# Retention scores per head over 64 rows in two banks, in place of zero-padded pairs

## The chip, the cores and the metric

One NeuronCore of one Trainium2 chip (1 of its 8) runs the whole block as a single program. The metric is device time in microseconds of one launch; lower is better.

## The reference

One layer of a hybrid backbone over 1024 tokens of width 1024, with 256 context tokens. One projection of the modulated, normalised input feeds two mixers, a gated long convolution (512 channels) and a retention with 8 heads of 64 channels in chunks of 128 tokens; their outputs go through one output projection, then a squared-ReLU MLP. The change lies in the retention:

```python
qc, kc, vc = ...            # (B, H, N chunks, C = 128, 64)
scores = jnp.einsum("bhncd,bhnmd->bhncm", qc, kc) * dmask[None, :, None]
out_inner = jnp.einsum("bhncm,bhnme->bhnce", scores, vc)
...
out_cross = jnp.einsum("bhncd,bhnde->bhnce", qc * w_q[None, :, None, :, None], s_prev)
return (out_inner + out_cross).reshape(B, H, L, dv)
```

## The kernel before, in words

The program is written with tiles drawn from pools; a scheduler orders the instructions of every engine by the tiles' dependencies, by priorities (`urgent()`, L187, raises one) and by when a buffer of a pool comes free. Nothing of the order around the change is written out by hand.

The stage in question comes in the middle of the run. Three kinds of work are interleaved in it. `split_mix` (L1051) loads the convolution's output (mraw), and splits it into a high and a low part (mx). `out_conv(d)` (L1060) projects it, 24 products of 512 columns per call into poh, written by `mm3` (L182 to 185), after which VectorE adds the result into XN (L1069). `retention(hh, n, ctr, gss)` (L1074) handles one chunk of 128 tokens for one group of four heads. It is called for hh in 0, 1 and n in 0 to 7, 16 chunks in all; behind every second chunk stands one call of `out_conv`, and behind every fourth a `group_norm` (L1120), whose transposes are pz and whose results mr. Later come the products por of the retention's half of the output projection; their weights are o2 and o3 (o3l is the low part of o3, made on VectorE at L1170).

One chunk of `retention` goes as follows. Four transposes (L1089) put q of four heads into the bank pqd. The input q2l holds each head's 64 channels twice (128 columns a head), so the transposed rows hold them in rows 0 to 63 and again in rows 64 to 127. VectorE multiplies the bank by the decay table into qw (L1092). ScalarE copies heads 0 and 2 into the upper 64 rows, heads 1 and 3 into the lower 64 rows of the buffer qz (L1094, L1095; it is part of sgqz), whose other halves were set to zero once, by two memsets (L1049). Two products of 128 rows and 256 columns (L1098) multiply the keys of a pair of heads (ktl, head 2p in rows 0 to 63, head 2p + 1 in rows 64 to 127) with it: the zeros keep the heads apart. The scores psc go through VectorE's mask multiply into sT (L1101). Sixteen products of half the columns (L1108) form the output po from sT and vtl and from qw and stl; VectorE takes the mean (mu, L1111), the centred values (ctrs, L1112) and, after ScalarE's square, the sums gss (L1116).

The PSUM banks come from pools with two buffers a tag: poh and por use the tag mm, pqd and psc the tag aux, po and pz the tag cv.

Of the kernel before, what the change touches and what calls it, by code (L numbers as in the profile page):

```python
# [13 lines left out]
ALU = mybir.AluOpType  # L14
# [3 lines left out]
P = 128  # L18
# [122 lines left out]
def tile_hymba_block(ctx: ExitStack, tc: tile.TileContext, I: dict, out: bass.AP, dbg=None, stop=99):  # L141
    nc = tc.nc
    V, A, G, PE, SP = nc.vector, nc.scalar, nc.gpsimd, nc.tensor, nc.sync
    dbg = dbg or (lambda name, ap: None)

    def bc(ap, k, shape):
        return ap.unsqueeze(k).broadcast_to(shape)
# [3 lines left out]
    def opool(key, bufs=1, **kw):  # L151
        st = ExitStack()
        es_open[key] = st
        return st.enter_context(tc.tile_pool(name=key, bufs=bufs, reuse_waits="tile", **kw))
# [21 lines left out]
    def ps_aux(name):  # L176
        return psB.tile([P, 512], F32, tag="aux", name=name)

    def ps_cv(name):
        return psB.tile([P, 512], F32, tag="cv", name=name)  # L180
# [6 lines left out]
    def urgent():  # L187

        return tc.high_priority(offset=6000)
# [52 lines left out]
    start = opool("start", side="right")  # L242
# [141 lines left out]
    for k in range(KC):  # L384
        for h in range(2):
# [9 lines left out]
            for i, (cv, w_) in enumerate(parts):  # L395
                for n in range(2):
                    PE.matmul(pga[h][0:4, n, :], lhsT=cv[:, k, :], rhs=w_[:, n * 512:(n + 1) * 512],  # L397
                              start=(k == 0), stop=(k == KC - 1 and i == 1))
# [120 lines left out]
    pr = ps_cv("prinv")  # L519
# [37 lines left out]
    def context(wh, wl, nm):  # L557
        ps = ps_aux(nm)
        pv = ps.rearrange("p (j n) -> p j n", n=256)
        for j in range(2):  # L560
            for k in range(KC):
                mm3(pv[:, j], hch[:, k, j * P:(j + 1) * P], hcl[:, k, j * P:(j + 1) * P],
                    wh[:, k], wl[:, k], k == 0, k == KC - 1)
        return pv
# [161 lines left out]
    wqT, msk = tab[:, 0], tab[:, 1]  # L726
# [15 lines left out]
    for hh in range(2):  # L742
        hs = slice(4 * hh, 4 * hh + 4)
        kr = kvp.tile([P, NCH, 256], F32, tag="kr", name=f"kr{hh}")
        wcur = slabs["k", hh]
        for g, ps in token_major(("k", hh), f"pk{hh}"):
# [4 lines left out]
            for m in range(2):  # L751
# [6 lines left out]
                kt = kvp.tile([P, 2, 256], F32, tag="kt", name=f"kt{hh}_{n0}")  # L758
                A.copy(kt.rearrange("p j n -> p (j n)"), pt)
                SP.dma_start(kT_d[hh][n0:n0 + 2].rearrange("j p n -> p j n"), kt)  # L760
        pc = context(*wcur, f"pck{hh}")
# [9 lines left out]
        for g, ps in token_major(("v", hh), f"pv{hh}"):  # L771
# [4 lines left out]
            for j in range(4):  # L776
                n = 4 * g + j
# [4 lines left out]
                for h in range(4):  # L782
                    for r in range(2):
                        PE.matmul(pt[64 * r:64 * r + 64, h * HD:(h + 1) * HD], lhsT=kw[:, h, r],
                                  rhs=vt[:, j, h * HD:(h + 1) * HD], start=True, stop=True)
                A.copy(Tt[0:64, n], pt[0:64, 0:256])
                A.copy(Tt[64:128, 7 - n], pt[64:128, 0:256])
        pc = context(*wcur, f"pcv{hh}")
# [4 lines left out]
        for h in range(4):  # L793
            for j in range(2):
                PE.matmul(pt[:, h * HD:(h + 1) * HD], lhsT=kwc[:, j, h].rearrange("p r d -> p (r d)"),
                          rhs=vc[:, j, h * HD:(h + 1) * HD], start=(j == 0), stop=(j == 1))
# [13 lines left out]
        for dr in range(2):  # L810
            rows = slice(64 * dr, 64 * dr + 64)
# [29 lines left out]
    for hv in range(2):  # L841
# [30 lines left out]
        for r, u in butterflies(cvp, scp, vT, 256, f"v{hv}"):  # L872
            nm = f"v{hv}{r}"
# [72 lines left out]
        for x, z in ((1, 7), (3, 5)):  # L946
            t = cvp.tile([P, 2, 256], F32, tag="pr1", name=f"sd{hv}{x}")
# [79 lines left out]
    def place(i, name, dt=F32R):  # L1027
        return big.tile([P, 4, 512], dt, tag=f"b{i}", name=name)
# [8 lines left out]
    wqT, msk = [tabq[:, 2 * i:2 * i + 2].rearrange("p a (h n) -> p (a h) n", n=P) for i in range(2)]  # L1037
# [3 lines left out]
    sgqz = place(12, "sgqz", F32)  # L1041
    sg = sgqz[:, 0:2].rearrange("p a n -> p (a n)").rearrange("p (j n) -> p j n", j=4)
    mraw = place(13, "mraw", F32)


    qz = [sgqz[:, 2 + i].rearrange("p (h n) -> p h n", h=4) for i in range(2)]
    with urgent():
        for t in qz:
            V.memset(t, 0.0)  # L1049

    def split_mix(k):  # L1051
        for q in range(2):
# [21 lines left out]
    def retention(hh, n, ctr, gss):  # L1074
        hs = slice(4 * hh, 4 * hh + 4)
        j = n % 4
        nm = f"{hh}_{n}"
        q2 = rtl.tile([P, 4, 2 * HD], F32, tag="q2", bufs=2, name=f"q2l{nm}")
        SP.dma_start(q2.rearrange("p h d -> p (h d)"), q2_d[hh][n])
        kt = rtl.tile([P, 2, P], F32, tag="ktl", bufs=2, name=f"ktl{nm}")  # L1080
        SP.dma_start(kt.rearrange("p a n -> p (a n)"), kT_d[hh][n])
        vt = rtl.tile([P, 256], F32, tag="vtl", bufs=2, name=f"vtl{nm}")
        SP.dma_start(vt, v_d[hh][n])
        st = rtl.tile([P, 256], F32, tag="stl", bufs=2, name=f"stl{nm}")
        SP.dma_start(st[0:64], st_d[hh][0, n])
        SP.dma_start(st[64:128], st_d[hh][1, 7 - n])
        pq = ps_aux(f"pqd{nm}")
        for h in range(4):
            PE.transpose(pq[:, h * P:(h + 1) * P], q2[:, h], ident)  # L1089
        pqv = pq.rearrange("p (h c) -> p h c", h=4)  # L1090
        qw = rtp.tile([P, 4, P], F32, tag="qw", bufs=2, name=f"qw{nm}")
        V.tensor_tensor(qw, pqv, wqT[:, hs], op=ALU.mult)  # L1092
        qT = qz[n % 2]
        A.copy(qT[0:64, 0:4:2], pqv[0:64, 0:4:2])  # L1094
        A.copy(qT[64:128, 1:4:2], pqv[64:128, 1:4:2])  # L1095
        pc = ps_aux(f"psc{nm}")
        for pr in range(2):
            PE.matmul(pc[:, pr * 256:(pr + 1) * 256], lhsT=kt[:, pr],  # L1098
                      rhs=qT[:, 2 * pr:2 * pr + 2].rearrange("p h c -> p (h c)"), start=True, stop=True)
        sT = rtp.tile([P, 4, P], F32, tag="sT", bufs=2, name=f"sT{nm}")  # L1100
        V.tensor_tensor(sT, pc.rearrange("p (h c) -> p h c", h=4), msk[:, hs], op=ALU.mult)  # L1101
        po = ps_cv(f"po{nm}")
        for h in range(4):
            cc = slice(h * HD, (h + 1) * HD)
            for w, o, first in ((sT, vt, True), (qw, st, False)):
                for r in range(2):
                    rows = slice(64 * r, 64 * r + 64)
                    PE.matmul(po[rows, cc], lhsT=w[:, h, rows], rhs=o[:, cc], start=first, stop=not first)  # L1108
        pov = po[:, 0:256].rearrange("p (h d) -> p h d", h=4)
        mu = rtp.tile([P, 4], F32, tag="mu", bufs=2, name=f"mu{nm}")  # L1110
        V.tensor_reduce(mu, pov, axis=AX.X, op=ALU.add)  # L1111
        V.scalar_tensor_tensor(ctr[:, j].rearrange("p (h d) -> p h d", h=4), bc(mu, 2, [P, 4, HD]), -1.0 / HD, pov,  # L1112
                               op0=ALU.mult, op1=ALU.add)
        sq = rtp.tile([P, 256], F32, tag="sqo", name=f"sqo{nm}")
        A.activation(sq, ctr[:, j], AF.Square)
        V.tensor_reduce(gss[:, j], sq.rearrange("p (h d) -> p h d", h=4), axis=AX.X, op=ALU.add)  # L1116
# [23 lines left out]
    for hh in range(2):  # L1140
        for g in range(2):
            ctr = ctrs[:, g]
            gss = rtp.tile([P, 4, 4], F32, tag="gss", bufs=2, name=f"gss{hh}{g}")
            for j in range(4):
                retention(hh, 4 * g + j, ctr, gss)
                if hh == 0 and g == 0 and j == 0:
                    for d in range(KC):
                        SP.dma_start(xn[d], I["xT"][d * P:(d + 1) * P])
                if j == 1 and pending:
                    group_norm(*pending)  # L1150
                if j == 1:
                    SP.dma_start(sg.rearrange("p n d -> p (n d)"), sg_d[hh][g])
                if j % 2:
                    out_conv(4 * hh + 2 * g + j // 2)
                if (hh, g, j) == (0, 0, 1):
                    prefetch()
                if (hh, g, j) == (0, 0, 3):
                    wo = [slab(I["w_out"][2], "o2", o2)]
                if (hh, g, j) == (1, 0, 0):

                    o3r = wpool.tile([P, 4, 512], F32, tag="wh", bufs=2, name="o3r")
                    SP.dma_start(o3r, I["w_out"][3])
            pending = hh, g, sg, ctr, gss
# [249 lines left out]
    def mlp1_step(f, c0, c1):  # L1413
        if f not in hid:
            if f % 2:
                hid[f] = [CH[:, i].rearrange("p (a n) -> p a n", a=2) for i in range(2)]
            else:
                hid[f] = [evs.tile([P, 2, 512], F32, tag=f"c{i}", name=f"c{i}_{f}") for i in range(2)]
        return dict(f=f, cols=slice(c0, c1), nm=f"1_{f}_{c0}")
# [4 lines left out]
    s = mlp1_step(0, 0, 256)  # L1424
# [5 lines left out]
    for f in range(NB):  # L1430
        with urgent():
            w1_load(f + 2)
        s = steps[f]
# [105 lines left out]
    for i, p in enumerate(TURNS[:-1]):  # L1539
        half, h = {1: (0, 0), 2: (0, 0), 5: (1, 1), 6: (0, 1), 3: (0, 1), 7: (1, 1)}[p]  # L1540
# [3 lines left out]
        for j in range(NG):  # L1544
            n = NG * i + j
            factors(n + AHEAD)
            t, w = TW.pop(n)
# [14 lines left out]
    n = NG * 6  # L1562
# [3 lines left out]
    for c, cols in enumerate(parts):  # L1566
        st = dict(ss=norms[0]["ss"][:, cols])
        for dp in range(4):
            db = slice(P * dp, P * dp + P)
            for j in range(NG):  # L1570
                t, w = TW[n + j]
# [25 lines left out]
```

## Time and profile before

| | |
|---|---|
| Time, three runs | 1373.8, 1377.99, 1381.97 us; median 1377.99 |
| Profiled execution | 1370.97 us, its span 1369.2 us |
| PE busy | 1294.8 us (95%) |
| VectorE (DVE) busy | 973.3 us (71%) |
| ScalarE (ACT) busy | 533.6 us (39%) |
| Retention stage, 15 of 16 chunks | 589.6 to 663.2 us |

How to read it: the times are of whole launches, the trace is of one of them. A row of a timeline gives start, duration, engine, line, operation and out<-in, with shapes; for matmuls "128\*128" is rows by columns of the array in use, and a product of f32 operands shows as two passes. Matmuls are pipelined, so a row's duration holds the way through the array; what a product takes from PE is the distance from its start to the next one's. A group of rows gives the count, the summed busy time and the mean of one in ns, then the idle time before them and what ended it.

### The profile page before, as it was taken

How to read it: one execution, taken by the hardware profiler on the slowest of the kernel's cores; microseconds unless marked ns; L12 is line 12 of the kernel's file. 1: busy time of each engine (PE TensorE's matmuls, PEld its weight loads, DVE VectorE, ACT ScalarE, POOL GpSimd, SP SyncE). 2: the span in 40 equal slices, each digit the busy share in tenths (PEclk: the TensorE clock that was granted, in tenths of full speed). 3: DMA queues.
4: the chain of work that ended last, by engine and by line, in shares of the span. 5: the costliest groups of instructions: out<-in, count | busy, mean ns of one | idle time of the engine just before them, and what ended most of it. 6: DMA issues, size and time to landing. Idle time of an engine off the chain costs nothing.

```text
span 1369.2 us, 20105 instructions
## 1 busy us (share of the span) xinstructions
PE 1294.8 (95%) x7386; PEld 1083.1 (79%) x7386; DVE 973.3 (71%) x1721; ACT 533.6 (39%) x912; POOL 19.4 (1%) x24
## 2 busy tenths in 40 slices
PE   6899899999999999799896999999998999999996
PEld 1479798988788999678776888888886888888896
DVE  5889787357878775558887988888656945555563
ACT  6863432213133121223455444444445744344420
POOL 0140000000000000000000000000000000000000
PEclk9799999999999999999998999999999999999999
DMA  9445766273536644776321789988636996666621
GB/s 374 175 151 160 233 206 212 79 228 129 169 120 215 206 162 155 270 243 182 104 96 64 251 306 326 348 302 300 238 123 232 338 321 190 193 201 185 199 79 62
DMA packets 139570, 278.19 MB, mean 203 GB/s; under 512 B 14672, under 2 KB 47056, under 8 KB 137040
## 3 DMA queue, kind: packets, MB, share of 16 engines
q1 hardware_dynamic: 137744, 272.19, 59.5%
q0 software_dynamic: 1152, 4.19, 0.8%
q8 instruction: 58, 0.95, 0.3%
q10 hardware_dynamic: 576, 0.52, 0.1%
q14 instruction: 40, 0.33, 0.1%
HBM read 193.75 MB, written 83.10 MB: 202 GB/s over the span
## 4 chain that ended last, share of the span: by engine, by line
PE 77%; DVE 8%; DMA 7%; ACT 4%; issue 2%; SPq 1%; POOL 0%; DVEq 0%; ACTq 0%; POOLq 0%
PE px L184 6%; PE px L185 6%; PE px L183 6%; PE pw L183 5%; PE py L183 5%; PE py L185 5%; PE py L184 5%; PE pw L185 5%; PE pw L184 5%; DMA dft_f_k<-in_dft_f 2%; PE pga L397 1%; PE pq L185 1%; PE pq L184 1%; PE pq L183 1%; PE pGv L901 1%
## 5 line engine op out<-in xcount | busy, mean ns | idle before, releaser
L1191 DVE TENSOR_TENSOR mt<-tr,mt 128x512 fp32r<-128x512 f32 x112 | 76.6, 688 | 99.6 <-ACT mt L1190 99.4
L1190 ACT CAST mt<-tr 128x512 fp32r<-128x512 f32 x112 | 69.6, 621 | 123.5 <-PE py L185 67.1
L183 PE MATMUL px<-mt,mw 128*128 128x512 f32 (+1 forms) x320 | 112.5, 352 | 3.0 <-ACT mw L1190 2.4
L184 PE MATMUL px<-mt,mw 128*128 128x512 f32 (+1 forms) x320 | 112.5, 352 | 0.7 <-DVE mt L1191 0.7
L185 PE MATMUL px<-mt,mw 128*128 128x512 f32 (+1 forms) x320 | 111.6, 350 | 0.0
L1191 DVE TENSOR_TENSOR mw<-wr,mw 128x512 fp32r<-128x512 f32 x112 | 76.6, 686 | 4.8 <-ACT mw L1190 4.4
L183 PE MATMUL py<-mt,mw 128*128 128x512 f32 x192 | 74.7, 389 | 0.0
L184 PE MATMUL py<-mt,mw 128*128 128x512 f32 x192 | 74.7, 389 | 0.0
L185 PE MATMUL py<-mt,mw 128*128 128x512 f32 x192 | 74.7, 389 | 0.0
L1190 ACT CAST mw<-wr 128x512 fp32r<-128x512 f32 x112 | 69.0, 617 | 9.8 <-DMA wr<-in_w_mlp 5.5
L183 PEld LDWEIGHTS px<-mt,mw 128*128 128x128 f32 x320 | 61.1, 191 | 11.4 <-ACT mw L1190 2.8
L184 PEld LDWEIGHTS px<-mt,mw 128*128 128x128 f32 x320 | 61.1, 191 | 9.2 <-DVE mt L1191 1.2
L185 PEld LDWEIGHTS px<-mt,mw 128*128 128x128 f32 x320 | 60.9, 191 | 8.2 <-DVE mw L1191 0.3
L183 PE MATMUL px<-hxh,wh_x 128*128 128x512 f32 x128 | 50.7, 396 | 0.0
L184 PE MATMUL px<-hxl,wh_x 128*128 128x512 f32 x128 | 50.6, 395 | 0.0
L185 PE MATMUL px<-hxh,wl_x 128*128 128x512 f32 x128 | 50.6, 395 | 0.0
L712 DVE SCALAR_TENSOR_TENSOR adac<-adaw,cs,adac 128x512 f32<-128x512 f32 x56 | 42.9, 766 | 9.8 <-DMA adaw<-in_w_ada 9.2
L185 PE MATMUL pk<-wh_k,hxl 128*128 128x256 f32 x128 | 39.2, 307 | 3.3 <-DVE hxl L438 3.3
L184 PEld LDWEIGHTS py<-mt,mw 128*128 128x128 f32 x192 | 36.0, 188 | 7.5
L183 PEld LDWEIGHTS py<-mt,mw 128*128 128x128 f32 x192 | 36.0, 188 | 7.5
L185 PEld LDWEIGHTS py<-mt,mw 128*128 128x128 f32 x192 | 36.0, 188 | 7.4
L183 PE MATMUL pk<-wh_k,hxh 128*128 128x256 f32 x128 | 39.6, 310 | 0.4 <-ACT hxh L434 0.4
(500 smaller groups left out, 3764.0 us busy)
## 6 DMA issues: line engine op xcount, KB each, us to landing
tr<-t_d SPq DMA_DIRECT2D x112, 256.0 KB, 4.0
adaw<-in_w_ada SPq DMA_DIRECT2D x64, 256.0 KB, 4.0
WH<-in_w_mlp SPq DMA_DIRECT2D x16, 1024.0 KB, 7.4
s_d<-WH SPq DMA_DIRECT2D x16, 1024.0 KB, 5.0
wr<-s_d SPq DMA_DIRECT2D x64, 256.0 KB, 4.0
wr<-in_w_mlp SPq DMA_DIRECT2D x48, 256.0 KB, 4.2
t_d<-c SPq DMA_DIRECT2D x40, 256.0 KB, 4.1
t_d<-CH SPq DMA_DIRECT2D x40, 256.0 KB, 5.4
```

The lines of the kernel that those rows point to most:

```text
L183: PE.matmul(o, lhsT=lh, rhs=rh, start=first, stop=False, **kw)
L184: PE.matmul(o, lhsT=lh, rhs=rl, start=False, stop=False, **kw)
L185: PE.matmul(o, lhsT=ll, rhs=rh, start=False, stop=last, **kw)
L397: PE.matmul(pga[h][0:4, n, :], lhsT=cv[:, k, :], rhs=w_[:, n * 512:(n + 1) * 512], start=(k == 0), stop=(k == KC - 1 and i == 1))
L712: V.scalar_tensor_tensor(ac, wa, cs[:, k, 0:1], ac, op0=ALU.mult, op1=ALU.add)
L901: PE.matmul(o, lhsT=y[:, 0, cb], rhs=iv[:, sl[0]], start=True, stop=False)
L1190: A.copy(hi, src)
L1191: V.tensor_tensor(lo, src, hi.bitcast(F32), op=ALU.subtract)
```

## The change

The copy of the transposed q becomes one copy of the whole bank, without zeros, so that the memsets go. The scores of each head are a product of their own: 64 rows of the keys by 64 rows of q, 128 columns. The even heads' products use rows 0 to 63 and write one bank, the odd heads' use rows 64 to 127 and write a second bank; in program order they alternate. The mask multiply becomes two operations on half the columns, one per bank. psc is now two allocations of the tag aux, so a chunk draws three from it in place of two.

```diff
-    qz = [sgqz[:, 2 + i].rearrange("p (h n) -> p h n", h=4) for i in range(2)]
-    with urgent():
-        for t in qz:
-            V.memset(t, 0.0)
+    qTs = [sgqz[:, 2 + i].rearrange("p (h n) -> p h n", h=4) for i in range(2)]
...
-        qT = qz[n % 2]
-        A.copy(qT[0:64, 0:4:2], pqv[0:64, 0:4:2])
-        A.copy(qT[64:128, 1:4:2], pqv[64:128, 1:4:2])
-        pc = ps_aux(f"psc{nm}")
+        qT = qTs[n % 2]
+        A.copy(qT, pqv)
+
+        pc = [ps_aux(f"psc{nm}{s}") for s in range(2)]
         for pr in range(2):
-            PE.matmul(pc[:, pr * 256:(pr + 1) * 256], lhsT=kt[:, pr],
-                      rhs=qT[:, 2 * pr:2 * pr + 2].rearrange("p h c -> p (h c)"), start=True, stop=True)
+            for s in range(2):
+                rows = slice(64 * s, 64 * s + 64)
+                PE.matmul(pc[s][:, pr * P:(pr + 1) * P], lhsT=kt[rows, pr], rhs=qT[rows, 2 * pr + s],
+                          start=True, stop=True)
         sT = rtp.tile([P, 4, P], F32, tag="sT", bufs=2, name=f"sT{nm}")
-        V.tensor_tensor(sT, pc.rearrange("p (h c) -> p h c", h=4), msk[:, hs], op=ALU.mult)
+        for s in range(2):
+            V.tensor_tensor(sT[:, s:4:2], pc[s][:, 0:256].rearrange("p (h c) -> p h c", h=2),
+                            msk[:, 4 * hh + s:4 * hh + 4:2], op=ALU.mult)
```

The order on PE, first in the second group of heads. Before, chunk 4 (psc_4, po_4), with the transposes of chunk 5 (pqd_5) and the projection products poh:

```order
L1098 MATMUL psc_4_6309<-sgqz,ktl_4_6293 128x256 [waits DMAHW0_49,PE_49,Activation_49]
L1098 MATMUL psc_4_6309<-sgqz,ktl_4_6293 128x256
L1089 MATMUL pqd_5_6346<-cols,q2l_5_6337 128x128 [waits DMAHW1_49,DVE_49]
L1089 MATMUL pqd_5_6346<-cols,q2l_5_6337 128x128 x3
L183 MATMUL poh_6527<-mx_5467,wh_o_5626 128x512
L184 MATMUL poh_6527<-mx_5468,wh_o_5626 128x512
L185 MATMUL poh_6527<-mx_5467,wl_o_5627 128x512
L1108 MATMUL po_4_6314<-vtl_4_6295,sT_4_6312 64x64 [waits DMAHW3_49,DVE_49]
```

With the change, chunk 2 of that group, from the third score product on, to chunk 3 (psc_30 and psc_31 are its two banks):

```order
L1096 MATMUL psc_20_6217<-sgqz,ktl_2_6202 128x128
L1096 MATMUL psc_21_6218<-sgqz,ktl_2_6202 128x128
L1108 MATMUL po_2_6226<-vtl_2_6204,sT_2_6223 64x64 [waits DMAHW7_49,DVE_49]
L1108 MATMUL po_2_6226<-vtl_2_6204,sT_2_6223 64x64
L1108 MATMUL po_2_6226<-stl_2_6206,qw_2_6214 64x64 [waits DMAHW1_49,DMAHW0_49]
L1108 MATMUL po_2_6226<-stl_2_6206,qw_2_6214 64x64
L1085 MATMUL pqd_3_6258<-cols,q2l_3_6249 128x128 [waits DMAHW2_49,PE_49]
L1108 MATMUL po_2_6226<-vtl_2_6204,sT_2_6223 64x64 [waits DVE_49]
```

```order
L1085 MATMUL pqd_3_6258<-cols,q2l_3_6249 128x128 x3
L1096 MATMUL psc_30_6266<-sgqz,ktl_3_6251 128x128 [waits DMAHW4_49,Activation_49]
L1096 MATMUL psc_31_6267<-sgqz,ktl_3_6251 128x128 [waits PE_49]
```

The next chunk's transposes have moved from between psc and po into and behind po, po stands in two pieces, of 4 and 12 products, and no poh stands between one chunk's scores and the next one's.

The order on SP's queue ahead of the stage (mraw are the loads of the mix, q_d the stores of q). Before:

```order
L1036 DMA tabq<-tab_d 128x2048 [waits DMAHW2_49]
L1055 DMA mraw<-mix_d_2960 128x512 [waits DMAHW3_49]
L1009 DMA q_d_4460<-q_5421 128x2x512 [waits DVE_49]
L1055 DMA mraw<-mix_d_2960 128x512 [waits DMAHW5_49]
L1055 DMA mraw<-mix_d_2961 128x512 [waits DMAHW6_49]
```

With the change:

```order
L1036 DMA tabq<-tab_d 128x2048 [waits DMAHW2_49]
L205 DMA wr_o_5636<-in_w_out 128x1024 [waits DMAHW7_49,DMAHW3_49,DVE_49]
L1009 DMA q_d_4460<-q_5421 128x2x512 [waits DVE_49]
L1051 DMA mraw<-mix_d_2960 128x512 [waits DMAHW5_49]
L1009 DMA q_d_4460<-q_5429 128x2x512 [waits DMAHW6_49,DVE_49]
L1051 DMA mraw<-mix_d_2960 128x512
```

The first load of the mix has moved from ahead of the q_d store to behind it.

The order on VectorE in the second group of heads, chunk 1 (sT_1). Before:

```order
L1101 TENSOR_TENSOR sT_1_6095<-psc_1_6092,tabq 128x512 [waits PE_49]
L1116 TENSOR_REDUCE gss_6025<-sqo_0_6069 128x4 [waits Activation_49]
L291 SCALAR_TENSOR_TENSOR rso_6121<-rs_to_6125,rs_yo_6122 128x16 [waits DVE_49]
L1092 TENSOR_TENSOR qw_2_6186<-pqd_2_6181,tabq 128x512 [waits PE_49]
L1127 TENSOR_TENSOR ctrs<-ctrs,rso_6121 128x1024 [waits DVE_49]
```

With the change:

```order
L1100 TENSOR_TENSOR sT_1_6122<-psc_10_6116,tabq 128x2x128 [waits PE_49]
L1170 TENSOR_TENSOR o3l<-o3r,o3h 128x1024 [waits DMAHW2_49,Activation_49]
L1065 SCALAR_TENSOR_TENSOR XN_5447<-poh_6573,mod_1379,XN_5447 128x1024 [waits PE_49]
L1170 TENSOR_TENSOR o3l<-o3r,o3h 128x1024 [waits Activation_49]
L1100 TENSOR_TENSOR sT_1_6122<-psc_11_6117,tabq 128x2x128
L1137 SCALAR_TENSOR_TENSOR mr_5460<-pz_6159,cols,mr_5459 128x512 [waits Activation_49]
L1088 TENSOR_TENSOR qw_2_6214<-pqd_2_6209,tabq 128x512 [waits PE_49]
```

Between the two halves of sT stand two operations on o3l and one on XN.

## Rows read from the trace of the kernel before

**Rows 1.** The page, busy time, share of the span and instructions of each engine.

```profile
PE 1294.8 (95%) x7386; PEld 1083.1 (79%) x7386; DVE 973.3 (71%) x1721; ACT 533.6 (39%) x912; POOL 19.4 (1%) x24
```

**Rows 2.** Windows: us, busy (x) of PE, PEld, DVE, ACT, POOL, clock, DMA share, GB/s.

```profile
555.00:563.30 8.30, 1.72 (x8) 0.80 (x6) 7.47 (x12) 1.86 (x3) 0.00 (x0) 0.85 0.47 158
...
589.60:663.20 73.60, 70.14 (x742) 55.11 (x740) 57.67 (x108) 26.10 (x58) 0.00 (x0) 1.00 0.56 170
```

**Rows 3.** Waits of PE, 589 to 700 us: total us, times, longest.

```profile
PE por L183 <- DVE XN L1258: 2.8, 1, 2.8
PE pqd L1089 <- DMA q2l<-q_d: 1.7, 1, 1.7
PE psc L1098 <- ACT sgqz L1095: 1.6, 2, 0.9
```

**Rows 4.** Timeline of PE, 616 to 618 us: start, us, engine, line, operation.

```profile
616.24 1.03 PE L1098 MATMUL psc<-sgqz,ktl 128*128 128x256 f32 x4
617.10 0.60 PE L1089 MATMUL pqd<-cols,q2l 128*128 128x128 f32 x4
```

**Rows 5.** Timeline of PE, 593 to 596 us, around one po.

```profile
593.44 0.39 PE L184 MATMUL poh<-mx,wh_o 128*128 128x512 f32 x1
593.67 0.39 PE L185 MATMUL poh<-mx,wl_o 128*128 128x512 f32 x1
593.99 0.34 PE L1108 MATMUL po<-vtl,sT 128*64 128x64 f32 x4
594.15 0.29 PE L1108 MATMUL po<-stl,qw 128*64 128x64 f32 x4
...
594.85 0.29 PE L1108 MATMUL po<-stl,qw 128*64 128x64 f32 x4
595.07 0.66 PE L1089 MATMUL pqd<-cols,q2l 128*128 128x128 f32 x4
```

**Rows 6.** Timeline of PE, 75.9 to 77.1 us, around a product of 64 rows.

```profile
75.95 0.39 PE L453 MATMUL peo<-fwh,hs 128*128 128x512 f32 x1
76.27 0.50 PE L454 MATMUL peo<-fwl,hs 64*128 64x512 f32 x1
76.70 0.39 PE L183 MATMUL pk<-wh_k,hxh 128*128 128x256 f32 x1
76.93 0.28 PE L184 MATMUL pk<-wl_k,hxh 128*128 128x256 f32 x1
```

**Rows 7.** Timeline of all engines, 572 to 577.1 us, one chunk's chain.

```profile
573.52 0.69 DVE L1092 TENSOR_TENSOR qw<-pqd,tabq 128x512 f32<-128x512 f32 x1 [0.93 <-PE pqd L1089]
...
574.25 0.37 ACT L1094 COPY sgqz<-pqd 64x256 f32<-64x256 f32 x1
...
575.06 1.13 PE L1098 MATMUL psc<-sgqz,ktl 128*128 128x256 f32 x4
576.23 0.69 DVE L1101 TENSOR_TENSOR sT<-psc,tabq 128x512 f32<-128x512 f32 x1 [1.30 <-PE psc L1098]
577.05 0.34 PE L1108 MATMUL po<-vtl,sT 128*64 128x64 f32 x4
```

**Rows 8.** Groups by form, DVE, 575 to 663.3 us: busy us, mean ns | idle before.

```profile
L1069 DVE SCALAR_TENSOR_TENSOR XN<-poh,mod,XN 128x1024 f32<-128x1024 f32 x8 | 10.2, 1281 | 5.5 <-PE poh L185 5.1 <-DMA XN<-in_xT 0.5
...
L1111 DVE TENSOR_REDUCE mu<-po 128x4 f32<-128x256 f32 x15 | 6.3, 421 | 5.3 <-PE po L1108 5.3
...
L1170 DVE TENSOR_TENSOR o3l<-o3r,o3h 128x1024 fp32r<-128x1024 f32 x2 | 2.4, 1220 | 0.0
```

**Rows 9.** Groups by form, 400 to 650 us: a copy of 512 columns and the memsets.

```profile
L903 ACT COPY Gs<-pGv 128x512 f32<-128x512 f32 x8 | 4.7, 583 | 31.5 <-PE pGv L902 31.5
...
L1049 DVE MEMSET sgqz<- 128x512 f32 x2 | 1.0, 485 | 0.1
```

**Rows 10.** Timeline of SP's queue, 550 to 560 us.

```profile
550.36 0.70 SPq L1055 DMA_DIRECT2D mraw<-mix_d  x1
558.66 0.37 SPq L1009 DMA_DIRECT2D q_d<-q  x1
```

## The prediction

> **What bounds the kernel now.** First the page's busy shares: PE is occupied for 95% of the span, VectorE for 71% [rows 1]. An average can hide a stage with another limit, so second the busy time by stretch [rows 2]. From 555.00 to 563.30 us PE works 1.72 of 8.30 us: it waits for the mix to come from memory. In the stretch that holds 15 of the 16 retention chunks (589.60 to 663.20) PE is busy for 70.14 of 73.60 us, VectorE for 57.67, ScalarE for 26.10. So PE bounds this stage, and anything that leaves PE without work is paid in full. Third, PE's waits from 589 to 700 [rows 3]: only three reasons count, 2.8 us for XN at the tail, 1.7 us for a load of q2l, 1.6 us in two waits of psc for the copies into sgqz. The chain from transposes through VectorE and ScalarE to the scores, five dependent steps per chunk, is covered by projection products (poh) that stand between them.
>
> **The change, part by part.** The sum is against the profiled execution, 1371.0 us, which lies 7 us under the median of the three runs, 1378.0. A measurement can tell about 0.5%, 6.9 us.
>
> *A. The score products themselves.* Before, the psc passes of a chunk take PE from 616.24 to 617.10, 0.86 us for two products of 256 columns, two passes each: 0.215 a pass [rows 4]. After, four products of 128 columns and 64 rows are eight passes of 0.107. One after the other they also take 0.86; two at a time, rows 0 to 63 beside rows 64 to 127, they take 0.43. No row of before shows halves by rows side by side; halves by columns are there: in po's middle six groups of four passes take 0.70 us from 594.15 to 594.85, 0.117 each, where four passes of 64 columns alone would be 4 × 0.215 × 64/256 = 0.215 [rows 5]. That is nearest, so I take 0.43 and one staggered pass, 0.54. Then there is the way in and out of the 64-row form. The one product of 64 rows in an otherwise full-row stream, peo at 76.27, lengthens three steps: from the peo ahead of it to the second pk behind it the starts are 0.32, 0.43 and 0.23 us apart [rows 6]. Without a change of form a product of 512 columns takes 0.23, as poh from 593.44 to 593.67 [rows 5], and one of 256 half of that, 0.12. So an excursion costs 0.98 − 0.58 = 0.40 us. A chunk becomes 0.54 + 0.40 = 0.94 against 0.86: +0.08, for 16 chunks **+1.3 us**. Bounds: perfect pairs 0.83, −0.5 us; no pairing 1.26, +6.4 us.
>
> Beside [rows 6]: the Trainium skill, TensorEngine Tiling (Array Packing), Key Properties, says that a change of tiling mode drains TensorE, which agrees with the 0.40; its Theoretical Speedup gives up to 2 times for a contraction of at most 64. By that table alone the step would be 16 × 0.43 = 6.9 us shorter; it is the rival "faster" below.
>
> *B. po torn in two.* The order shows that in 13 of 16 chunks po's first four products now run as soon as the first half of sT is there and the other twelve come later, with one to four other products between. Each tear is one more excursion into the half-column form. Its price from rows: into po, 0.32 for the last poh instead of 0.23 and 0.16 for the first group instead of 0.117; out of it, 0.22 instead of 0.117 [rows 5]: 0.09 + 0.04 + 0.10 = 0.24 us. In eight of them PE has other work beside it: 8 × 0.24 = **+1.9 us** (0 if free, 4.6 if the tear costs what the 64-row form costs and all 13 pay: 13 × 0.35).
>
> *C. Steps with nothing beside them.* The buffers decide this. The tag aux has two. Before, a chunk drew two from it, pqd and psc, so the next pqd was transposed right behind psc. Now a chunk draws three: psc's second bank takes pqd's own buffer, and the next pqd must wait for the first half of sT. The chain turns serial, and from chunk 2 to 5 of the second head group (three steps) no poh or por is left to cover it. One step, by [rows 7] and [rows 8]: scores start at 0; the bank's last pass leaves at 0.32, its result lies 0.27 later (psc's row lasts 1.13 and takes 0.86), so 0.59. VectorE starts 0.04 later and needs some 0.42 for 256 columns, as mu does: 1.05. po starts 0.13 later (576.92 to 577.05), 1.18. Eight passes 0.23 and a switch 0.05, the first transpose 0.3, twelve products 0.70: 2.5. The other three transposes end by 3.1 (four last 0.6). VectorE has finished mu by then; qw, 0.69, to 3.8; the copy of 512 columns starts 0.04 later and takes 0.58 [rows 9]: 4.45; 0.04 later the next scores. PE is without work from 0.64 to 1.18 and from 2.9 to 4.5: 2.1 us. Three steps: **+6.3 us** (5 with copy and qw side by side in part, 7.5 if each switch adds 0.4).
>
> *D. The second half of sT in VectorE's queue.* In the second group's chunk 1, two o3l of 1.22 us and an XN of 1.28 now stand between the halves of sT: 3.7 us [rows 8]. po's rest waits behind them. PE has pz's transposes, one round of pqd and eleven por meanwhile, some 2.5 us, so it stands for about 1.5, less 0.3, and 0.7 more at qw behind it. In chunk 5 the half's 0.5 and the waits of the last group norm (mr, pz) give about 1.5. Together **+3.7 us** (2 to 5).
>
> *E. Waits that go.* psc's 1.6 us for the copies: where it stood there are now seven to eleven poh ahead of psc: **−1.6** (0 to −1.6). The wait for q2l is a transfer and stays. The tail's 2.8 for XN stays in my sum: its last products again follow the same XN; if the slack swallows it, −2.8.
>
> *F. The start of the stage.* The two memsets, 0.97 us of VectorE [rows 9], go. Without them the scheduler also orders SP's queue otherwise: the first mix load, issued at 550.36 ahead of the q_d write, now stands behind that write, which is issued at 558.66 when its data are ready [rows 10]. PE loses the poh products that it did in 555 to 563, and in the order 25 instead of 36 poh stand ahead of the first scores: eleven of 0.23 us, 2.5 us of work, are pushed to later, less the half microsecond that VectorE gets back. **+2.0** (0 to +4).
>
> *One copy instead of two* (0.58 for two of 0.37) lies on ScalarE, busy for 26.10 of 73.60 us, and its gain of 0.16 per chunk counts only where the chain is bare, in C.
>
> **Sum:** +1.3 + 1.9 + 6.3 + 3.7 − 1.6 + 2.0 = +13.6 us: 1384.6 against 1371.0; set on the median, 1378 + 13.6, **1391 us** (+1%). With all lower bounds −0.5 + 0 + 5 + 2 − 1.6 − 2.8 + 0 = +2; with all upper 6.4 + 4.6 + 7.5 + 5 + 4 = +27.
>
> **Rivals.** *No pairing*: the halves by rows run one after the other. Then A is +6.4, the sum +18.7, 1397 us. For it: no row shows row halves together. Against it: the columns' halves do [rows 5]. The Trainium skill, TensorEngine Tiling (Array Packing), Gotcha 1, lets row tiles run together only if they write to different banks, which this change does; no row of before shows it. *No change*: PE's new pauses lie ahead of the tail's 2.8 us for XN [rows 3] and of loads, and what PE loses in C it would have waited later; poh moved into the chunks fill the others. Then +2 to +5, about 1381. Against it: only 6.1 us of such waits exist at all. *Faster*: the 0.40 of [rows 6] is due to the weights of that one product, a switch of row form costs under 0.25 us, pairs run fully, and por fill the bare steps. Then 16 × −0.43 = −6.9, memsets −1, waits −1.6 and some of 2.8: about −9 to −10, 1369 us. The point from which it decides is the step's total: 0.43 plus the switch must stay below 0.86 by more than what C and D put back, which needs their 10 us to be almost wholly covered.
>
> **How the numbers follow.** The forecast (+7 to +20) has 0.60, of which 0.09 lies in its lower tail within 0.5%; no pairing 0.14; no change 0.18; faster 0.08. So slower by over 0.5%: 0.51 + 0.14 = 0.65; within: 0.27; faster: 0.08. The range goes from the lower bounds' sum, 1379, to 1403; it leaves out the faster case and the corner where all upper bounds meet.
>
> **What would show it.** Right: psc's eight passes take about 0.5 us with starts in pairs; psc's start to the next start in chunks 2 to 5 of the second group about 4.5 us, PE's waits there for qw or the copy some 1.6 us each and for sT 0.5; po in two pieces; the wait for the second half of sT in chunk 1; first poh near 564. Wrong: PE's idle time from 589 to 663 staying near 3.5 us would fell C and D; psc passes spaced 0.107 without overlap would show no pairing; a gap at the switch under 0.1 would make A −4 us or better.

## The result, and the profile after

The change takes 1392.4 us (median of 8 runs, 1388.8 to 1399.0) against 1376.8 us before (8 runs, 1372.8 to 1385.0): a ratio of 1.0115, 95% interval 1.0091 to 1.0139. That is slower by 15.6 us, clear of noise, and 1.4 us from the 1391 forecast. The total of the forecast was nearly right; several of its terms were not, and that their errors cancel is luck, as the account below shows.

The page of the changed kernel, engines, beside [rows 1]:

```profile
PE 1304.7 (94%) x7450; PEld 1088.0 (78%) x7450; DVE 974.9 (70%) x1735; ACT 528.4 (38%) x896; POOL 19.5 (1%) x24
```

The profiled execution has a span of 1389.4 us, 20.2 more than before. A part of that cannot be laid to the change: the last product of the projection ahead of the stage, pq, starts at 555.35 us before and at 562.01 after, though PE's order is the same up to there. A second profile of the changed kernel has it at 558.74, and in the profiles of the experiments below it starts anywhere from 552.7 to 565.4. So I compare the stage from its own ends, from the last pq to the last row of ptr (722.38 before, 740.18 after). Busy time by stretch, before and after (columns as in [rows 2]):

```profile
555.35:575.06 19.71, 12.39 (x44) 8.33 (x42) 14.04 (x21) 7.66 (x12) 0.00 (x0) 0.83 0.68 216
575.06:663.20 88.14, 84.68 (x832) 67.00 (x831) 63.31 (x115) 26.51 (x59) 0.00 (x0) 1.00 0.64 207
663.20:722.38 59.18, 53.96 (x267) 44.12 (x262) 50.70 (x79) 29.91 (x48) 0.00 (x0) 0.97 0.31 107
```

```profile
562.01:581.53 19.52, 10.06 (x32) 6.59 (x30) 12.71 (x19) 7.43 (x11) 0.00 (x0) 0.65 0.72 231
581.53:651.88 70.35, 70.33 (x637) 53.69 (x636) 47.77 (x90) 16.45 (x29) 0.00 (x0) 1.00 0.64 213
651.88:662.82 10.94, 6.06 (x89) 4.46 (x88) 6.21 (x14) 2.53 (x6) 0.00 (x0) 0.87 0.43 116
662.82:669.38 6.56, 4.64 (x44) 3.49 (x44) 5.05 (x13) 1.12 (x4) 0.00 (x0) 0.50 0.33 103
669.38:677.58 8.20, 7.62 (x55) 5.91 (x55) 4.88 (x10) 2.42 (x5) 0.00 (x0) 0.53 0.50 152
677.58:740.18 62.60, 57.37 (x346) 46.29 (x345) 53.88 (x87) 30.47 (x50) 0.00 (x0) 1.00 0.29 101
```

The stage takes 178.17 us in place of 167.03: +11.1. The medians differ by 15.6; the other 4.5 us lie outside the stage, and no run here says whether they are the change's. The stage's loss sits in the short rows in the middle. From 651.88 to 662.82 PE works 6.06 of 10.94 us, and from then to 677.58 it does run, but at a granted clock of 0.50 and 0.53, the lower of its two levels (1.2 in place of 2.4 GHz). From 581.53 to 651.88, the first ten chunks, PE is full.

A step from one chunk's scores to the next one's is called bare here when no projection product stands in it to cover the chain. One of them, from the scores of the second group's chunk 3 to those of chunk 4:

```profile
657.61 0.72 PE L1096 MATMUL psc<-sgqz,ktl 64*128 64x128 f32 x8 [1.40 <-ACT sgqz L1090]
658.35 0.76 DVE L1100 TENSOR_TENSOR sT<-psc,tabq 128x256 f32<-128x256 f32 x2
658.83 0.34 PE L1108 MATMUL po<-vtl,sT 128*64 128x64 f32 x4 [0.51 <-DVE sT L1100]
659.22 0.33 PE L1085 MATMUL pqd<-cols,q2l 128*128 128x128 f32 x1
659.47 0.34 PE L1108 MATMUL po<-vtl,sT 128*64 128x64 f32 x4
...
660.52 0.90 PE L1085 MATMUL pqd<-cols,q2l 128*128 128x128 f32 x3
661.46 0.69 DVE L1088 TENSOR_TENSOR qw<-pqd,tabq 128x512 f32<-128x512 f32 x1 [0.40 <-PE pqd L1085]
662.18 0.58 ACT L1090 COPY sgqz<-pqd 128x512 f32<-128x512 f32 x1 [4.31 <-DVE qw L1088]
662.82 1.22 PE L1096 MATMUL psc<-sgqz,ktl 64*128 64x128 f32 x8 [1.40 <-ACT sgqz L1090]
```

That is the chain of the forecast, link by link: 0.51 us of idle PE for the first half of sT, po in two pieces round one transpose, 1.40 for qw and the copy. PE's waits in the stage say how often:

```profile
PE poh L183 <- ACT mx L1053: 9.5, 2, 9.1
PE psc L1096 <- ACT sgqz L1090: 4.2, 3, 1.4
PE por L183 <- DVE XN L1258: 3.4, 3, 1.7
PE po L1108 <- DVE sT L1100: 3.1, 4, 1.6
```

Against [rows 3], psc waits three times 1.40, and po 3.1 us for sT, which did not wait before. The transfer wait for q2l is gone.

### The profile page after: what moved, and what is told of

Same layout as the page of the kernel before. It is cut to its first block, busy times and chain, and to the rows that moved or that the text cites. A ratio compares the mean times of both kernels' runs of the same rounds, so it can differ in the third digit from the quotient of the medians.

```text
span 1389.4 us, 20234 instructions
## 1 busy us (share of the span) xinstructions
PE 1304.7 (94%) x7450; PEld 1088.0 (78%) x7450; DVE 974.9 (70%) x1735; ACT 528.4 (38%) x896; POOL 19.5 (1%) x24
## 4 chain that ended last, share of the span: by engine, by line
PE 71%; DVE 11%; DMA 9%; ACT 4%; issue 3%; SPq 1%; POOL 0%; DVEq 0%; ACTq 0%; POOLq 0%
PE px L184 6%; PE px L185 6%; PE px L183 6%; PE py L184 4%; PE py L185 4%; PE py L183 4%; PE pw L183 4%; PE pw L185 3%; PE pw L184 3%; PE po L1108 2%; PE pga L397 1%; PE poh L183 1%; PE poh L185 1%; PE pGv L901 1%; PE pq L183 1%
```

## The experiments

Each is compared with the kernel before on its own chip, so ratios are compared, not times.

**Is it the look-ahead?** The second bank comes from the tag cv:

```diff
-        pc = [ps_aux(f"psc{nm}{s}") for s in range(2)]
+        pc = [ps_aux(f"psc{nm}0"), ps_cv(f"psc{nm}1")]
```

> The change, but the second score bank is drawn from the tag cv, so that aux again gives the next chunk's transposes their buffer early; the products of 64 rows stay. Theory 1 (the lost look-ahead costs: 7.3 us of PE's idle time in the bare steps, and the half clock from about 660 to 677 us that follows them, some 5): the bare steps and that half clock vanish, the time falls by about 10 to 13 us, from 1392 to 1379 to 1382. Rival (the products of 64 rows cost, by switches of form): it stays at 1388 to 1394.

Measured: 1378.2 us, ratio 1.0019 (0.9998 to 1.0040). Nearly the whole loss goes, with the products of 64 rows still in. PE's wait for the copy, 4.2 us after, is down to one:

```profile
PE psc L1096 <- ACT sgqz L1090: 0.7, 1, 0.7
```

The stage is 167.9 us, and there is no half clock between 573 and 733 us. So the third draw from aux decides, by itself or by the order that comes of it; that does not say yet whether 64 rows gain.

**The buffers without the 64 rows.** The change, with the products over 128 padded rows:

```diff
-        A.copy(qT, pqv)
+        A.copy(qT[0:64, 0:4:2], pqv[0:64, 0:4:2])
+        A.copy(qT[64:128, 1:4:2], pqv[64:128, 1:4:2])
...
-                PE.matmul(pc[s][:, pr * P:(pr + 1) * P], lhsT=kt[rows, pr], rhs=qT[rows, 2 * pr + s],
+                PE.matmul(pc[s][:, pr * P:(pr + 1) * P], lhsT=kt[:, pr], rhs=qT[:, 2 * pr + s],
```

with the memsets back.

> The change's two banks, two halves of sT and three draws from aux, but with the zero-padded products over 128 rows (two copies, memsets) in place of 64 rows. Theory 1 (64 rows save some 0.2 us a chunk, 3 to 4 us in all, and the buffers cost): slower than the change by 0 to 4 us after the front's 2 to 4 us are taken off, 1390 to 1396, with psc at about 0.86 us of PE a chunk and the same bare steps. Rival (the 64-row form costs): faster than the change, 1380 to 1386.

Measured: 1385.7 us, 1.0070 (1.0046 to 1.0093): faster than the change, so theory 1 missed here. The scores do cost more: between two poh they take 1.12 us of PE (median of nine places) against 0.85. But the waits are smaller:

```profile
PE psc L1100 <- ACT sgqz L1093: 1.8, 3, 1.2
...
PE po L1112 <- DVE sT L1104: 0.8, 1, 0.8
```

and the clock stays full through the bare steps (no half clock from 571 to 741 us). The longer scores fill time in which PE would stand anyway. So the rival was right on the time and not on the reason: between two poh the 64-row form itself is the cheaper one, by 0.27 us a chunk. The memsets are not the reason either: put back alone, they gain nothing (next run). What this run cannot separate is the part of the clock from that of another order on VectorE.

**The front.** The change with the memsets put back, which restores the first mix load's place:

```diff
     qTs = [sgqz[:, 2 + i].rearrange("p (h n) -> p h n", h=4) for i in range(2)]
+    with urgent():
+        for t in qTs:
+            V.memset(t, 0.0)
```

> The change with the two memsets put back (their zeros are overwritten), which gives SP's queue the order of before: the first mix load ahead of the q_d store. Theory 1 (the front is a part of its own, worth 2 to 4 us, by eleven products of 0.23 us and less idle time ahead of the first poh): 1388 to 1390, 29 and 7 poh ahead of the first scores. Rival (the front is hidden by later waits): 1391 to 1394.

Measured: 1391.7 us, 1.0111 (1.0079 to 1.0143): no gain. The first poh does start 1.9 us behind the last pq again, in place of 9.4, and 36 poh stand ahead of the first scores, which come 19.4 us behind the last pq, as they did. But those poh are then missing later: PE now stands in a fourth step too (1.0 us for sT at 647.76), and the half clock lasts 23.9 us from about 654. So the front is paid back, as far as one profile tells, and that one is of the longest of the six runs (1398.3 us).

Then both edits, the bank from cv and the memsets:

> Both: the second bank from cv and the memsets back. Theory 1: the sum of the two steps, 1374 to 1379, at or a little under the kernel before, with psc at about 0.5 us in place of 0.86 a chunk as what is left of the change. Rival (64 rows cost): 1385 to 1392.

Measured: 1382.8 us, 1.0035 (1.0012 to 1.0057), so the two steps do not add. Its interval overlaps that of the first experiment, so it is not shown to be slower than that one either. Its stage is 167.6 us, as long as there. In the two profiles the difference lies ahead of the stage: the last pq starts at 561.86 in place of 557.21 us, and up to there PE is busy for 525.1 in place of 521.0 us on the same products. Why, these runs do not show.

**Filling the bare steps.** 14 products of 256 columns for each of the second group's chunks 2 to 5:

```diff
+        po = ps_cv(f"po{nm}")
+        if hh == 1 and 2 <= n <= 5:
+            for i in range(14):
+                PE.matmul(po[:, 256:512], lhsT=mx[0][0][:, 0, 0:P], rhs=mx[0][0][:, 1, 0:256], start=True, stop=True)
```

> The change with 14 products of 256 columns added to each of the second group's chunks 2 to 5, written to the unused half of po's bank and read by nobody; they wait for no result of the chain and fall into the bare steps. Added work 56 x 0.107 = 6 us, against some 8 us in which PE stands there. Theory (half the clock loss of these steps comes from PE standing: the granted clock of 0.5 from about 660 to 677 us doubles what PE does there): the clock stays at full speed, the stage is 3 to 6 us shorter though it does more, 1386 to 1389. Rival (the clock falls for other reasons, or does not matter): the half clock stays and the time is the change's or more, 1392 to 1398.

Measured: 1387.4 us, 1.0085 (1.0064 to 1.0106). The stretch of the bare steps:

```profile
650.00:677.00 27.00, 25.30 (x291) 19.86 (x291) 18.61 (x39) 6.97 (x13) 0.00 (x0) 1.00 0.37 109
```

PE is busy for 25.30 of 27.00 us at full clock. With work in the gaps the clock does not fall, so its fall in this stretch follows from PE standing, as far as one profile with the fill shows. The stage, however, is as long as without the fill (178.2 against 178.2 us), not 3 to 6 us shorter. What is shown is that 6 us of added work cost nothing there; that the total gains is not, as the two intervals overlap.

**The tears of po.** po's heads in the order 0, 2, 1, 3, with the bank from cv and without:

```diff
-        for h in range(4):
+        for h in (0, 2, 1, 3):
             cc = slice(h * HD, (h + 1) * HD)
```

> The second bank from cv as before, and po's heads in the order 0, 2, 1, 3, so that po's first eight products need only the first half of sT. Theory (each tear of po costs about 0.24 us, some ten of them go): 2 to 3 us under the run with cv alone (1378.2), 1375 to 1376.5, level with the kernel before. Rival (the tears are free): 1378.

Measured: 1377.0 us, 1.0014 (0.9996 to 1.0033). The step of 1 us is too small against the intervals to tell.

The second, without the bank from cv:

> The change as it is, with po's heads in the order 0, 2, 1, 3 alone: aux still gives three buffers a chunk and the bare steps stay. Theory (look-ahead and clock are the cost, tears 2 to 3 us): 1389 to 1390, with the half clock near 660. Rival (the tears are the main cost): 1382 or less.

Measured: 1387.1 us, 1.0073 (1.0050 to 1.0095): 2 to 3 us better than expected, but not 1382. po's slots in the stage fall from 21.2 to 18.3 us (the distances from each start to the next, less recorded idle time), but not all of that is the tears: at full clock a torn po takes 1.23 us in its own rows and a whole one 1.08, and 4.7 us of po's slots ran at half clock with the change, 1.9 here. About half of the 2.9 us is each. psc's wait for the copy rises to 6.9 us, for the steps stay bare; yet the half clock, near 666, is only 6.8 us long.

**Do the halves by rows run side by side?** First their order, so that both products of rows 0 to 63 come first:

```diff
-        for pr in range(2):
-            for s in range(2):
+        for s in range(2):
+            for pr in range(2):
```

> The change with both products of rows 0 to 63 first, then both of rows 64 to 127. Theory (the 0.43 us of the eight passes comes from neighbours in the queue that use different rows): only the pass at the seam pairs, psc takes about 0.75 to 0.86 and its step 1.2 to 1.3 in place of 0.85, so +5 to +7 us where PE is full and less in the bare steps: 1395 to 1399. Rival (PE takes the halves side by side in any order): 1392 and psc at 0.43.

Measured: 1383.4 us, 1.0051 (1.0030 to 1.0073). My theory fell: the scores still take 0.65 us to the next start. The scheduler puts out another order all the same (all four transposes between po's pieces in five steps, where the change has one), and psc waits 1.4 us for the copy in place of 4.2. Then all four on the same rows:

```diff
-                PE.matmul(pc[s][:, pr * P:(pr + 1) * P], lhsT=kt[rows, pr], rhs=qT[rows, 2 * pr + s],
+                PE.matmul(pc[s][:, pr * P:(pr + 1) * P], lhsT=kt[0:64, pr], rhs=qT[0:64, 2 * pr + s],
```

> The change with all four score products on rows 0 to 63 (the odd heads' scores come from the even rows' data, so the output is not the reference's); number and size of the passes stay. Theory (two row halves work side by side): with one half alone the eight passes are spaced 0.107 us, 0.86 us from the first psc to what follows at least, in place of 0.65. Rival (a pass of 64 rows simply takes half as long): 0.65 as in the change.

Measured: ratio 1.0161 (1.0119 to 1.0202), two runs of a kernel that leaves out the odd heads' own rows. Scores between two poh: before, after, and with one half of the rows, each a timeline of PE:

```profile
591.44 0.40 PE L183 MATMUL poh<-mx,wh_o 128*128 128x512 f32 x1
591.78 1.13 PE L1098 MATMUL psc<-sgqz,ktl 128*128 128x256 f32 x4
592.56 0.58 PE L184 MATMUL poh<-mx,wh_o 128*128 128x512 f32 x1
592.98 0.40 PE L185 MATMUL poh<-mx,wl_o 128*128 128x512 f32 x1
```

```profile
598.71 0.40 PE L184 MATMUL poh<-mx,wh_o 128*128 128x512 f32 x1
599.04 0.72 PE L1096 MATMUL psc<-sgqz,ktl 64*128 64x128 f32 x8
599.68 0.50 PE L185 MATMUL poh<-mx,wl_o 128*128 128x512 f32 x1
600.02 0.40 PE L183 MATMUL poh<-mx,wh_o 128*128 128x512 f32 x1
```

```profile
593.22 0.40 PE L184 MATMUL poh<-mx,wh_o 128*128 128x512 f32 x1
593.55 1.16 PE L1096 MATMUL psc<-sgqz,ktl 64*128 64x128 f32 x8
594.63 0.50 PE L185 MATMUL poh<-mx,wl_o 128*128 128x512 f32 x1
594.97 0.40 PE L183 MATMUL poh<-mx,wh_o 128*128 128x512 f32 x1
```

From the start of the first poh to that of the last, less 0.23 for each of two poh, the step costs 1.08 us before, 0.85 after, and 1.29 on one half. The difference of the last two, 0.44, is four passes of 0.107: rows 0 to 63 and 64 to 127 do work side by side, in either order of the queue. The single passes show it too: with the change they start in pairs 0.007 us apart (at 599.04, 599.25, 599.36 and 599.47), with one half first in pairs 0.014 us apart, and on one half one by one, 0.11 us apart. The Trainium skill, TensorEngine Tiling (Array Packing), Key Properties, states that different tiles can execute in parallel; these rows agree.

**The change again, and its order alone.** The same kernel a second time, and then one line that raises the transposes:

> The change itself once more, beside the runs below on one chip, with a second profile. Theory (the bare steps, the half clock behind them): 1390 to 1394, again a stretch at half clock that begins in chunk 2 or 3 of the second group, 10 to 20 us long. Rival (the half clock of the first profile was an accident of one execution): no such stretch, and the stage, from the last pq to the last ptr, near 173 in place of 178 us.

Measured: 1389.9 us, 1.0113 (1.0085 to 1.0140). The second profile has the same waits and the half clock again, 13.7 us of it from 653.4 and 3.4 more from 670.5, and a stage of 180.0 us. The clock falls there already behind the first of the bare steps' waits, 1.58 us for sT that end at 651.74:

```profile
PE psc L1096 <- ACT sgqz L1090: 4.7, 4, 1.4
```

```profile
653.00:673.00 20.00, 13.99 (x148) 10.66 (x143) 11.58 (x27) 2.92 (x7) 0.00 (x0) 0.60 0.41 125
```

```diff
-        for h in range(4):
-            PE.transpose(pq[:, h * P:(h + 1) * P], q2[:, h], ident)
+        with urgent():
+            for h in range(4):
+                PE.transpose(pq[:, h * P:(h + 1) * P], q2[:, h], ident)
```

> The change with one line: the four transposes of pqd get a raised priority, so they stand ahead of po in nearly every chunk; buffers, products and copies are those of the change. Theory (what costs is that three transposes stand behind po, which leaves qw and the copy bare, and that fillers are then used up): no bare steps, no half clock in the stage, few tears, stage 165 to 169 us, 1375 to 1380. Rival (the third draw from aux itself costs, for pqd must wait for the first half of sT in any place): PE waits 0.3 to 0.5 us at each pqd, 1383 to 1387.

Measured: 1379.4 us, 1.0056 (1.0033 to 1.0079): by the ratios about half of the loss goes with one line, the buffers untouched. The stage is 169.2 us with no half clock between 568 and 687. A chunk of it, where after had the bare steps:

```profile
642.38 0.40 PE L184 MATMUL poh<-mx,wh_o 128*128 128x512 f32 x1
642.71 0.71 PE L1097 MATMUL psc<-sgqz,ktl 64*128 64x128 f32 x8
643.35 0.50 PE L185 MATMUL poh<-mx,wl_o 128*128 128x512 f32 x1
643.69 0.40 PE L183 MATMUL poh<-mx,wh_o 128*128 128x512 f32 x1
643.93 0.66 PE L1086 MATMUL pqd<-cols,q2l 128*128 128x128 f32 x4
644.52 0.34 PE L1109 MATMUL po<-vtl,sT 128*64 128x64 f32 x4
```

Two poh cover the first half of sT, and po covers qw and the copy. The third draw from aux itself shows as one recorded wait in the whole stage:

```profile
PE pqd L1086 <- DVE sT L1101: 1.3, 1, 1.3
```

So a third buffer a chunk is dear only where the order leaves its wait bare. The last version adds to the raised transposes the heads' order and the halves in turn:

> The same with raised transposes, po's heads in the order 0, 2, 1, 3, and the products of rows 0 to 63 ahead of those of rows 64 to 127: of all versions the one whose fillers are spread most evenly. Theory: 0 to 2 us under the run before it, 1374 to 1378, so not clear of the kernel before. Rival: 1380 or more, if the late poh push the tail.

Measured: 1375.7 us against 1374.1 before, 1.0015 (0.9998 to 1.0031). Its stage, 164.7 us, is 2.3 shorter than that of the kernel before, but the whole run is not faster. No version of this study beats the kernel before.

## Why the prediction held, point by point

The stage's +11.1 us by what PE did (distances between starts, less recorded idle time, added up from the timelines of PE; before and after in us):

```
psc 14.1 -> 11.6    po 17.3 -> 21.2    pqd 5.8 -> 9.7    pz 3.2 -> 4.5
poh 52.9 -> 51.9    por 47.7 -> 47.4   others 10.3 -> 9.9
idle 15.8 -> 22.0   sum 167.1 -> 178.2
```

These rows hold the half clock too: after, 2.4 us of psc's, 4.7 of po's, 3.1 of pqd's and 1.8 of pz's ran at the lower level, before none of them.

*A, the scores: wrong sign.* The forecast was +1.3; psc's own rows fall by 2.5. The pairing and the switch were right (0.43 and, as 0.85 − 0.43, 0.42 for the 0.54 and 0.40 taken). The step that failed is "A chunk becomes 0.54 + 0.40 = 0.94 against 0.86": I charged the new form with its way in and out and the old one with none. Between two poh the old product, two-pass f32 among one-pass projections, takes 1.08, not 0.86. But in eleven of the 16 chunks of before, transposes follow the scores, and the two share one way in and out; around [rows 4]:

```profile
616.00 0.40 PE L185 MATMUL poh<-mx,wl_o 128*128 128x512 f32 x1
...
617.46 0.47 PE L183 MATMUL poh<-mx,wh_o 128*128 128x512 f32 x1
617.77 0.39 PE L184 MATMUL poh<-mx,wh_o 128*128 128x512 f32 x1
```

From 616.00 to 617.77, less two poh of 0.23, scores and transposes cost 1.31 together; after, scores cost 0.85 and transposes on their own, from 578.12 to 579.03 counted in the same way, 0.45. There the new form gains next to nothing. It gains 0.23 only in the four chunks whose scores stood alone: about 1 us in all, an estimate from these rows. The rest of psc's gain comes back in pqd's rows, whose +3.9 had no term in the forecast: about 1.5 of it is the half clock, the rest the way in and out that is no longer shared, and tears that hold a transpose.

*B, the tears: too small.* +1.9 forecast (its upper end was worked out with 0.35 a tear, though the price it names, that of the 64-row form, was 0.40). One tear with a poh in it:

```profile
583.00 0.29 PE L1108 MATMUL po<-stl,qw 128*64 128x64 f32 x4
583.22 0.50 PE L183 MATMUL poh<-mx,wh_o 128*128 128x512 f32 x1
583.65 0.34 PE L1108 MATMUL po<-vtl,sT 128*64 128x64 f32 x4
583.82 0.29 PE L1108 MATMUL po<-stl,qw 128*64 128x64 f32 x4
```

From 583.00 to 583.82 it takes 0.82 us, against 0.117 + 0.23 + 0.117: 0.36 and not 0.24, for the poh inside pays too (0.43 in place of 0.23). Thirteen of them are 4.6 us at most, the forecast's upper end. Eight of the tears hold one transpose instead; they cost 0.30, as po and the four transposes take 1.97 us torn and 1.67 whole.

*C, the bare steps: right.* Forecast 2.1 us of idle PE a step in three steps; measured 0.51 + 1.40 = 1.91 from chunk 3 to 4 and again from 4 to 5. From 2 to 3 the first wait is longer, which is D's.

*D: right in its sum's sign only.* The second half of sT did wait behind the two o3l and XN, and it cost nothing, as eleven por covered it: po's rest starts at 650.44, with no wait for sT. Instead the next chunk's first half stood behind mr and gss, and po waited 1.6 us at 654.17:

```profile
650.44 0.34 PE L1108 MATMUL po<-vtl,sT 128*64 128x64 f32 x4
...
652.71 0.75 DVE L1137 SCALAR_TENSOR_TENSOR mr<-pz,cols,mr 128x512 fp32r<-128x512 f32 x1 [0.42 <-ACT mr L1136]
653.38 0.41 DVE L1116 TENSOR_REDUCE gss<-sqo 128x4 f32<-128x256 f32 x1
...
654.17 0.34 PE L1108 MATMUL po<-vtl,sT 128*64 128x64 f32 x4 [1.58 <-DVE sT L1100]
```

That is 1.1 more than C's 0.5; with the 0.5 in chunk 5, 1.6 in all. Forecast 3.7 (its two parts, 1.9 and 1.5, make 3.4).

*E:* psc's old waits went, as forecast; the wait for q2l, which was to stay, went too, another −1.7. The tail's wait for XN stayed (3.2 before, 3.4 after).

*F, the front: as forecast inside the stage, yet nothing is won by restoring it.* The first scores come as long behind the last pq as before (19.5 against 19.7 us) with eleven poh fewer done, 2.5 us of work, and PE stands for 9.5 in place of 7.3 us ahead of them (2.7 of the 7.3 for VectorE's rpq, not for the mix that the forecast names); but with the front restored the total did not move.

*Not in the sum: the clock.* 17.1 us of the stage from about 660 ran at the lower level. Of the rows above, the step from 662.82 to 669.38 takes 6.56 us; at full clock one put together from its neighbours takes 1.22 (657.61 to 658.83) and 3.44 (654.17 to 657.61), 4.66. That is 1.9 us for one step. PE's 7.6 busy us from 669.38 to 677.58 lose at most 3.8 more. By these rows the errors in A, D and E, some 7.5 us too much in the sum, and those in B and the clock, up to 2.7 and up to 6 too little, nearly cancel. That is luck: the chain without cover was seen rightly, but the clock's fall was not, and the sum of +13.6 meets a stage of +11.1 and 4.5 us outside it that no term was about.

What the rivals said: no pairing is ruled out by the run on one half of the rows, and "no change" (+2 to +5) by the interval, which begins at 1.0091, 12.5 us. "Faster" had a gain per scores that exists only between two poh, 0.2 us, and failed, as the forecast put it, because the bare steps were not covered; with them covered the stage comes out 2.3 us shorter at best.

## What to carry to other kernels

When a change draws one more buffer a round, look for what can no longer be started early, and then whether the order leaves that wait bare: here one raised priority took back half of the loss, and one draw from another pool nearly all. Price the way in and out of a form on both sides of a change, also of the form that is removed, and look which neighbours share it. And look at where the fillers run out: work pushed later can be the cover that keeps PE, and its clock, up.

## What the runs showed that I had not expected

PE's clock fell to half among the bare steps: in both profiles of the change in the first or second of them, for some 17 us, and in three variants in the first to the fourth, for 6.8 to 24 us. It stayed full when products that nobody reads filled the gaps. And two halves of the rows run side by side even when the queue holds both products of one half first (0.65 us from psc to the next start in either order, 1.08 on one half alone).
